# A two-layer decoder trunk on one core: values products set three score blocks back, the norm factors' read-back queued behind transposes, a second raw weight buffer, and the value bounds summed in two slices

## The chip, the core and the metric

The kernel runs on one core of a Trainium2 chip. TensorE (PE) does the matrix products, VectorE (DVE), ScalarE (ACT) and GpSimd (POOL) the elementwise work, and SyncE (SP) issues every DMA of this kernel from one queue. Each engine takes its instructions strictly in the order in which they stand, so an instruction that waits holds up all that is behind it, and that goes for SP's queue of DMAs too. The metric is the device time of the whole program in microseconds, median of three runs, lower is better.

## The reference, cut to what matters

```python
def short_conv_mixer(h, w_in, w_out, conv_w):          # layer 0
    b_gate, c_gate, u, z = jnp.split(h @ w_in, 4, axis=-1)
    conv = causal_conv3(c_gate * u, conv_w)
    return (b_gate * conv * jax.nn.silu(z)) @ w_out

def diff_attn_mixer(h, w_in, w_out, ...):              # layer 1: 8 heads, each of two maps
    q, k, v, z = jnp.split(h @ w_in, 4, axis=-1)
    ...
        logits = jnp.einsum('bqhd,bkhd->bhqk', q_blk, k) * scale
        logits = jnp.where(dist >= 0, logits + bias, -jnp.inf)
        p = jax.nn.softmax(logits, axis=-1)            # 16 maps
        a = p[:, :, 0] - lam * p[:, :, 1]
        o = jnp.einsum('bhqk,bkhe->bqhe', a, v)
        return rmsnorm(o, subln_g) * (1.0 - lambda_init)
    ...
    return (o * jax.nn.silu(z)) @ w_out

for i in range(2):                                     # then a final rmsnorm
    x = x + (short_conv_mixer, diff_attn_mixer)[i](rmsnorm(x, norm_g[i]), ...)
```

The sequence has 1024 tokens, the model 1024 features, all in float32.

## The kernel before, in words

Activations lie with features on partitions, as eight chunks of 128 features by 1024 tokens. A float32 product is taken as three products of high and low parts (`mm3`, line 125: `wh*xh`, `wh*xl`, `wl*xh`). A weight unit of 128 x 1024 is loaded as `wr` (SP), rounded to `wh` by ACT (line 118), and `wl = wr - wh` is left to POOL (line 119); there is one `wr` buffer, and two each of `wh` and `wl`.

Layer 0 (lines 207 to 376) is one long run of products. Layer 1 works head by head. For a head h and a query block b of 128 queries, called block (h,b) below, `scores` (line 489) does this: PE takes the scores of both maps against the keys 0 to (b+1)*128 (line 511); DVE adds the bias (514) and takes the row maximum (516); ACT takes the exponentials into `p1` and `p2` (518); DVE joins the two maps (525); ACT rounds the result to a float16 high part (530, 531 or 534), and POOL (532, for b of 5 and more) or DVE (535) leaves the low part; SP issues one transposing DMA of both (537), out of `p2`'s memory into `p1`'s. `p1` comes from a ring of five slots, `p2` from a ring of three. The score banks in PSUM are two.

`values` (540) takes a group of two blocks: PE multiplies the transposes with the values' high and low parts into the one bank `av` (551), and DVE moves it to `o` (556). After two groups, `head_norm` (558) computes the norm factors of 512 tokens: ACT squares `o` (562), POOL splits the squares (146, 147), PE sums them over the partitions (`cps`, 156), DVE and POOL make the factor `rr` (567, 568), and it goes through memory: SP writes 512 single elements to `rrd` (571) and reads them back to every partition as `rb` (573); POOL multiplies `o` by `rb` (575), two blocks of scores later in the program.

Beside the attention of head h, the projections of the next head fill PE: k and q (`proj_qk`), the gate z of the last head (`proj_z`, whose store of `o` to `yd` at line 406 frees `o`'s slot; there are two), and the values of the next pair of heads (`proj_v`, whose first part bounds each value feature by a sum of squares in `aux`, lines 446 to 463). The instructions are put in order when the program is built, by a list scheduler with priorities (attention stands 4000 ahead of the projections) that simulates the engines' times. So the order on each engine is fixed, and a projection's products (a filler, below) stand where the scheduler expected PE to wait. At the end come the output projection, the residual and the final norm.

Of the kernel before, what the change touches and what calls it, by code (L numbers as in the profile page):

```python
# [15 lines left out]
I32 = mybir.dt.int32  # L16
# [20 lines left out]
class Ring:  # L37
    """Slots of one pool, taken in turn."""
# [4 lines left out]
    def tile(self, shape, dtype, name):  # L43
        tag = self.tags[self.n % len(self.tags)]
        self.n += 1
        return self.pool.tile(shape, dtype, tag=tag, name=name)
# [3 lines left out]
def trunk(ctx: ExitStack, tc: tile.TileContext, a: dict, out: bass.AP):  # L50
# [10 lines left out]
    sl = ctx.enter_context(tc.tile_pool(name="sl", bufs=1))      # slots of 4 KB a partition  # L61
# [12 lines left out]
    r_p1, r_p2, r_w = ring("pa", 5), ring("pb", 3), ring("w", 1)  # L74
    y_tags = r_k.tags + r_q.tags + r_v.tags + r_p2.tags
    free = r_z.tags + r_p1.tags + r_w.tags
# [27 lines left out]
    # the tensor engine's clock is up before the first operands are there  # L104
# [6 lines left out]
    def unit(src, dst=None, raw=None, gain=None):  # L111
        """A weight unit [p, k * 128 + f], times a gain by p, as its high and low parts."""
        wr = wp.tile([P, D], F32, tag="wr", bufs=1, name="wr") if raw is None else raw
# [11 lines left out]
    def mm3(ps, wh, wl, rh, rl, ranges, ks=range(KC)):  # L125
        """ps[:, o] (+)= sum_k w[k].T @ r[k][:, t] for the (o, t, size) given."""
# [15 lines left out]
    def bf16_parts(sq, r1, r2, engs):  # L142
        """sq as the exact sum of three bfloat16 parts; the upper half of a float32 is its first 8 bits."""
# [6 lines left out]
    def col_sums(parts, n):  # L150
        """[p, b] = the sum of the parts' column of token b * 128 + p."""
# [8 lines left out]
    def norm_cols(sqs, n, rdst, tmp=None):  # L160
        """rdst[p, b] = rsqrt(mean_d x^2 + eps) of token b * 128 + p, from column sums of sqs."""
# [9 lines left out]
    def spread(r, tiles, eng):  # L171
        """Diagonal blocks of r's high and low parts."""
# [9 lines left out]
    def rows(tiles, n, at=None):  # L182
        """Every partition: the diagonals, one behind the other."""
# [6 lines left out]
    def norm_rows(rsrc, dst, n, tags):  # L190
        """dst[:, t] = r of token t on every partition, n blocks of 128 tokens at most 4 a step."""
# [19 lines left out]
    # the first three units (c, u, z) go k by k as x and they arrive  # L211
# [58 lines left out]
    # units come as (c, u, z, b) of each chunk of 128 features  # L270
# [48 lines left out]
    # relative bias less its far value, by distance + 127; masked past the diagonal  # L319
# [12 lines left out]
    # lambda, and the scale C that keeps the attention differences in float16's range  # L332
# [23 lines left out]
    # output projection, residual, and the split of the next layer's input  # L356
# [223 lines left out]
    def attention(h):  # L580
# [3 lines left out]
        for i, g in enumerate(order(h)):  # L584
# [3 lines left out]
            if i % 2 == 0 and norms:  # L588
                next(norms.pop())
# [165 lines left out]
```

## Time and profile before

| | us |
|---|---|
| device time, median of 3 runs | 1201.77 |
| lowest and highest | 1200.87, 1205.01 |
| span of the profiled execution | 1207.0 |
| layer 0 and its output projection | 0 to 458 |
| norm and first projections of layer 1 | 458 to 494 |
| attention, from the first scores to the last | 494 to 1073 |
| last values, output projection and final norm | 1073 to 1207 |

The profile is of one execution. No time beside its span is given for it, so the span is its own time here; it is 5.2 us (0.4%) above the median of the three runs. A granted clock of 1.0 is 2.4 GHz for TensorE, 0.5 is 1.2 GHz. Waits are read thus: the engine and line that waited, the engine and line that released it, the total, the times, the longest. In the timeline a number in square brackets is the idle time of that engine ahead of the row, with its releaser. SPq is SP's queue.

### The profile page before, as it was taken

Reading aid. Unit: us, or ns where it says so; the run is one execution under the profiler, and the core shown is the slowest. Engines: PE = TensorE matmul, PEld = TensorE weight load, DVE = VectorE, ACT = ScalarE, POOL = GpSimd, SP = SyncE. Lnnn points to the kernel's source line nnn. Section 1 sums busy time; section 2 is a strip of 40 time slices with the busy share of each in tenths; the row PEclk is TensorE's granted clock in tenths of the full one; section 3 lists DMA queues with packets and bytes.
Section 4 is the critical chain, followed back from the end, with each engine's and each line's share of the span. In section 5 each row is a group of like instructions: output and inputs, shape, how many; then the busy total and the mean of one; then the engine's idle time right before and its main releaser. Section 6 shows DMA issues by size and latency. Waiting matters only on the chain.

```text
span 1207.0 us, 15391 instructions
## 1 busy us (share of the span) xinstructions
PE 1072.0 (89%) x5960; PEld 899.9 (75%) x5960; DVE 590.7 (49%) x945; ACT 421.9 (35%) x705; POOL 563.5 (47%) x355
## 2 busy tenths in 40 slices
PE   8899999999999998996789867998879777888987
PEld 6778888888888886886678656886677666666786
DVE  6563222322323224873587636766385652785123
ACT  3211111101112232463464534545345343355232
POOL 7553424424423552464464545546436554443253
PEclk9899999999999998998989989998889888987989
DMA  5211111111113440356263443534545446457222
GB/s 178 85 53 53 53 53 38 50 53 53 48 40 110 157 140 35 95 81 131 60 150 76 101 105 86 128 89 103 120 95 88 97 112 127 101 119 208 53 105 97
DMA packets 124825, 112.41 MB, mean 93 GB/s; under 512 B 89248, under 2 KB 97104, under 8 KB 124752
## 3 DMA queue, kind: packets, MB, share of 16 engines
q1 hardware_dynamic: 124752, 111.42, 36.3%
q8 instruction: 47, 0.77, 0.3%
q14 instruction: 26, 0.21, 0.1%
HBM read 67.82 MB, written 12.12 MB: 66 GB/s over the span
## 4 chain that ended last, share of the span: by engine, by line
PE 56%; DMA 16%; POOL 9%; issue 8%; DVE 7%; ACT 3%; SPq 0%; POOLq 0%; DVEq 0%; ACTq 0%
PE big L131 34%; PE mm L131 14%; DMA rrd<-rr 7%; DMA p<-p 3%; DMA rb<-rrd 3%; PE sc L511 3%; PE av L551 2%; POOL wl L119 1%; POOL p L532 1%; POOL o L575 1%; DVE nm L516 1%; DVE aux L452 1%; POOL acc L660 1%; DMA yr<-yd 1%; DVE p L525 1%
## 5 line engine op out<-in xcount | busy, mean ns | idle before, releaser
L119 POOL TENSOR_TENSOR wl<-wr,wh 128x1024 fp32r<-128x1024 f32 x75 | 184.1, 2454 | 275.6 <-ACT wh L118 270.4
L118 ACT ACTIVATE wh<-wr 128x1024 fp32r<-128x1024 f32 x75 | 79.3, 1058 | 370.5 <-PE big L131 307.6
L131 PE MATMUL mm<-xh,wh 128*128 128x512 f32 (+1 forms) x432 | 172.0, 398 | 13.3 <-ACT xh L627 6.1
L131 PE MATMUL mm<-xl,wh 128*128 128x512 f32 (+1 forms) x432 | 171.6, 397 | 2.2 <-POOL xl L628 2.2
L131 PE MATMUL mm<-xh,wl 128*128 128x512 f32 (+1 forms) x432 | 170.4, 396 | 0.0
L131 PE MATMUL big<-xh,wh 128*128 128x512 f32 x464 | 143.8, 391 | 2.2 <-DVE cr L288 2.2
L131 PE MATMUL big<-xh,wl 128*128 128x512 f32 x464 | 143.7, 390 | 0.0
L131 PE MATMUL big<-xl,wh 128*128 128x512 f32 x464 | 143.5, 391 | 0.0
L551 PE MATMUL av<-p,vt 128*128 128x128 f16 x864 | 72.4, 249 | 69.2 <-DMA p<-p 52.4
L518 ACT ACTIVATE p<-sc,nm 128x256 f32<-128x256 f32 (+7 forms) x128 | 93.8, 736 | 95.9 <-DVE nm L516 80.0
L551 PEld LDWEIGHTS <-vt 128*128 128x128 f16 x864 | 61.9, 113 | 81.0 <-issue 56.1
L131 PEld LDWEIGHTS mm<-xh,wh 128*128 128x128 f32 x432 | 84.7, 196 | 29.3 <-ACT xh L627 6.5
L131 PEld LDWEIGHTS big<-xh,wh 128*128 128x128 f32 x464 | 87.3, 188 | 20.6 <-issue 2.6
L511 PE MATMUL sc<-kt,qt 128*128 128x512 f32 (+2 forms) x384 | 94.0, 368 | 9.6 <-DMA qt<-qt 5.5
L131 PEld LDWEIGHTS big<-xh,wl 128*128 128x128 f32 x464 | 87.6, 189 | 18.2
L131 PEld LDWEIGHTS big<-xl,wh 128*128 128x128 f32 x464 | 87.4, 188 | 18.2
L131 PEld LDWEIGHTS mm<-xl,wh 128*128 128x128 f32 x432 | 84.9, 196 | 18.2 <-POOL xl L628 3.1
L131 PEld LDWEIGHTS mm<-xh,wl 128*128 128x128 f32 x432 | 84.6, 196 | 15.1
L575 POOL TENSOR_TENSOR o<-o,rb 128x512 f32<-128x512 f32 x16 | 20.7, 1294 | 158.0 <-DMA rb<-rrd 145.6
L516 DVE TENSOR_REDUCE nm<-sc 128x2 f32<-128x256 f32 (+5 forms) x96 | 90.7, 950 | 1.1
L511 PEld LDWEIGHTS sc<-kt,qt 128*128 128x128 f32 x384 | 68.9, 201 | 19.9 <-ACT p L518 5.7
L478 PE MATMUL mm<-wl,xh 128*128 128x256 f32 x256 | 73.1, 287 | 1.8 <-POOL wl L119 1.8
(174 smaller groups left out, 1997.7 us busy)
## 6 DMA issues: line engine op xcount, KB each, us to landing
wr<-in_w_in SPq DMA_DIRECT2D x53, 512.0 KB, 3.5
wr<-in_w_out SPq DMA_DIRECT2D x16, 512.0 KB, 4.4
qt<-qt SPq DMA_DIRECT2D x32, 256.0 KB, 3.7
xr<-in_xT SPq DMA_DIRECT2D x15, 512.0 KB, 4.5
wr<-in_w_v SPq DMA_DIRECT2D x14, 512.0 KB, 4.0
x2d<-x SPq DMA_DIRECT2D x8, 512.0 KB, 2.8
kt<-lo SPq DMA_DIRECT2D x32, 128.0 KB, 3.0
rb<-rrd SPq DMA_DIRECT2D x16, 256.0 KB, 5.7
```

The source lines that it names most:

```text
L118: A.activation(out=wh, in_=wr, func=AF.Copy)
L119: G.tensor_tensor(out=wl, in0=wr, in1=f(wh), op=ALU.subtract)
L131: T.matmul(ps[:, o:o + n], lhsT=w[:, s], rhs=r[k][:, t:t + n], start=(k == 0 and r is rh and w is wh), stop=(k == KC - 1 and w is wl))
L452: V.tensor_tensor(out=sq if k == KC - 1 else aux[:, k % 4, :], in0=aux[:, (k - 1) % 4, :], in1=aux[:, k % 4, :], op=ALU.add)
L478: T.matmul(pt[:, i, :], lhsT=xh[k][:, ts], rhs=wl[:, kk], start=False, stop=False)
L511: T.matmul(sc[:, i, c0:c1_], lhsT=qt[:, var, ts], rhs=kt[:, c0:c1_], start=(var == 0), stop=(var == 1))
L516: V.tensor_reduce(out=nm[:, ms], in_=sc[:, :, :L], axis=AX, op=ALU.max, negate=True)
L518: A.activation(out=(p1_, p2_)[m][:, :L], in_=sc[:, i, :L], func=AF.Exp, bias=nm[:, m:m + 1], accum_out=st[:, m:m + 1])
L525: V.scalar_tensor_tensor(out=p1_[:, :L], in0=p2_[:, :L], scalar=cs[:, 1:2], in1=p1_[:, :L], op0=ALU.mult, op1=ALU.add)
L532: G.tensor_tensor(out=al, in0=p1_[:, :L], in1=ah, op=ALU.subtract)
L551: T.matmul(av[:, qi * P:(qi + 1) * P], lhsT=v[:, kb, es], rhs=at[:, r, :], start=(kb == 0 and r == 0 and v is vh), stop=(kb == qb and v is ...
L575: G.tensor_tensor(out=o, in0=o, in1=rb, op=ALU.mult)
```

## The change

Four things are changed, all in layer 1; comments and docstrings are also gone, so line numbers move by one to some twenty.

- `values` and what hangs on it (the norm steps) become `attend`, which is called when the first block of the second group after is scored, and its products are tied on PE behind the last score product of that block (`issue_after` adds an order on the same engine, no wait on another). So three blocks of scores stand between a group's last block and its values. The last two groups are attended after the last head's scores, with the same priority.
- The read-back of `rb` is issued at the second norm step, behind the last transposing DMA that the program has issued by then, in place of directly behind the write of `rrd`.
- `wr` has a second buffer from the start of layer 1 to the output projection, in the 4 KB that `aux` had.
- `aux` is two slices, not four: the running sum stays in slice 0, each new square goes to slice 1. It shares the slot `dgl` with a norm tile, and its result `srow` has a slot of its own.

```diff
@@ Ring.tile
-        return self.pool.tile(shape, dtype, tag=tag, name=name)
+        pool, tag = tag if isinstance(tag, tuple) else (self.pool, tag)
+        return pool.tile(shape, dtype, tag=tag, name=name)
...
-    r_p1, r_p2, r_w = ring("pa", 5), ring("pb", 3), ring("w", 1)
+    r_p1, r_p2, r_wr = ring("pa", 5), ring("pb", 3), Ring(wp, ["wr0"])
     y_tags = r_k.tags + r_q.tags + r_v.tags + r_p2.tags
-    free = r_z.tags + r_p1.tags + r_w.tags
+    free = r_z.tags + r_p1.tags + [(wp, "wr1")]
...
@@ unit
-        wr = wp.tile([P, D], F32, tag="wr", bufs=1, name="wr") if raw is None else raw
+        wr = r_wr.tile([P, D], F32, name="wr") if raw is None else raw
...
@@ ahead of layer 1
+    r_wr.tags.append("wr1")
     heads = [dict() for _ in range(NH)]
...
@@ proj_v
-            aux = r_w.tile([P, 4, 256], F32, name="aux")
+            aux = sm.tile([P, 2, 256], F32, tag="dgl", name="aux")
             sq = sm.tile([P, 256], F32R, tag="sqw", name="sq")
             for k in range(KC):
-                A.activation(out=aux[:, k % 4, :], in_=f(ws[k // 4][0])[:, (k % 4) * 256:(k % 4 + 1) * 256],
+                A.activation(out=aux[:, min(k, 1), :], in_=f(ws[k // 4][0])[:, (k % 4) * 256:(k % 4 + 1) * 256],
                              func=AF.Square, scale=g_sb[:, 1, k:k + 1])
                 if k:
-                    V.tensor_tensor(out=sq if k == KC - 1 else aux[:, k % 4, :], in0=aux[:, (k - 1) % 4, :],
-                                    in1=aux[:, k % 4, :], op=ALU.add)
+                    V.tensor_tensor(out=sq if k == KC - 1 else aux[:, 0, :], in0=aux[:, 0, :], in1=aux[:, 1, :], op=ALU.add)
...
-            srow = aux[:, 0, :]
-            half = aux[:, 1, :].bitcast(I32)            # half of n's biased exponent
+            srow = sm.tile([P, 256], F32, tag="srow", name="srow")
+            half = aux[:, 1, :].bitcast(I32)
...
-            sd = aux[:, 2, :].rearrange("p (a b) -> p a b", b=P)
+            sd = aux[:, 0, :].rearrange("p (a b) -> p a b", b=P)
...
+    turned = []
@@ scores
-                        T.matmul(sc[:, i, c0:c1_], lhsT=qt[:, var, ts], rhs=kt[:, c0:c1_],
-                                 start=(var == 0), stop=(var == 1))
+                        hd["last", qb] = T.matmul(sc[:, i, c0:c1_], lhsT=qt[:, var, ts], rhs=kt[:, c0:c1_],
+                                                  start=(var == 0), stop=(var == 1))
...
-        dma(out=at[:, :2 * qb + 2, :], in_=p16[:, :2 * L], transpose=True)
+        turned.append(dma(out=at[:, :2 * qb + 2, :], in_=p16[:, :2 * L], transpose=True))
...
@@ head_norm
             dma(out=rrd[h, half].rearrange("(b p) -> p b", p=P), in_=rr)
+        yield
+
         rb = sm.tile([P, 512], F32, tag="dgh", name="rb")
-        dma(out=rb, in_=rrd[h, half].unsqueeze(0).partition_broadcast(P))
-        yield
+        with tc.issue_after(turned[-1].ins):
+            dma(out=rb, in_=rrd[h, half].unsqueeze(0).partition_broadcast(P))
         G.tensor_tensor(out=o, in0=o, in1=rb, op=ALU.mult)
         yield
 
-    norms = []
+    norms, behind = [], []
+
+    def attend(h, i, g):
+
+        values(h, g)
+        if i % 2 == 0 and norms:
+            next(norms.pop())
+        if i % 2:
+            norms.append(head_norm(h, g // 2))
+            next(norms[-1])
...
@@ attention
                 scores(h, g, qi)
-            values(h, g)
-            if i % 2 == 0 and norms:
-                next(norms.pop())
-            if i % 2:
-                norms.append(head_norm(h, g // 2))
-                next(norms[-1])
+
+                if qi == 0 and len(behind) == 2:
+                    with tc.issue_after(heads[h]["last", 2 * g].ins):
+                        attend(*behind.pop(0))
+            behind.append((h, i, g))
...
@@ behind the last head
+    with tc.high_priority(offset=AHEAD):
+        while behind:
+            attend(*behind.pop(0))
     next(norms.pop())
...
+    r_wr.tags.pop()
-    wtags = [None] * 4 + r_v.tags[:2] + q7 + r_k.tags[2:] + r_w.tags + r_p2.tags
+    wtags = [None] * 4 + r_v.tags[:2] + q7 + r_k.tags[2:] + [(wp, "wr1")] + r_p2.tags
...
```

What the scheduler makes of it is seen in the order of the built programs. POOL around the low part of block (2,7), the last of head 2 (`p_4978` before, `p_4942` now; `rr` and `o<-o,rb` are the norm of its first half); before:

```order
L532 TENSOR_TENSOR p_4948<-p_4947,p_4948 128x896
L568 TENSOR_TENSOR rr<-rr,neghalf 128x4
L119 TENSOR_TENSOR wl<-wr,wh 128x1024
L430 TENSOR_TENSOR lo<-tq,kt 64x512
L575 TENSOR_TENSOR o<-o,rb 128x512
L532 TENSOR_TENSOR p_4978<-p_4977,p_4978 128x1024
L437 TENSOR_TENSOR qt<-tq,qt 64x512 x2
```

and now:

```order
L535 TENSOR_TENSOR p_4866<-p_4865,p_4866 128x896
L571 TENSOR_TENSOR rr<-rr,neghalf 128x4
L439 TENSOR_TENSOR qt<-tq,qt 64x512 x2
L535 TENSOR_TENSOR p_4942<-p_4941,p_4942 128x1024
L120 TENSOR_TENSOR wl<-wr,wh 128x1024
L439 TENSOR_TENSOR qt<-tq,qt 64x512 x2
L407 TENSOR_TENSOR o<-o,th 128x512
L120 TENSOR_TENSOR wl<-wr,wh 128x1024
L535 TENSOR_TENSOR p_5345<-p_5344,p_5345 128x896
L407 TENSOR_TENSOR o<-o,th 128x512
L580 TENSOR_TENSOR o<-o,rb 128x512
```

The multiplication by `rb` stood ahead of the block's low part; it now stands behind it, with six further rows between.

SP at the same place, where `p_4977` (before) and `p_4941` (now) are the transposes of block (2,7); before:

```order
L537 DMA_TRANSPOSE p_4947<-p_4948 128x14x128
L571 DMA rrd<-rr 128x4x1
L573 DMA rb<-rrd 128x512
L114 DMA wr<-in_w_v 128x1024
L431 DMA kt<-lo 64x512 x2
L537 DMA_TRANSPOSE p_4977<-p_4978 128x16x128
L438 DMA qt<-qt 64x2x512 x2
```

and now:

```order
L540 DMA_TRANSPOSE p_4865<-p_4866 128x14x128
L574 DMA rrd<-rr 128x4x1
L440 DMA qt<-qt 64x2x512 x2
L540 DMA_TRANSPOSE p_4941<-p_4942 128x16x128
L115 DMA wr<-in_w_in 128x1024
L440 DMA qt<-qt 64x2x512 x2
```

The read-back `rb` stood directly behind the write `rrd`, ahead of a weight load, two moves of `kt` and the transposes. Now the transposes follow the write, and this factor's read-back is the eighth row behind it, behind the transposes of block (3,6).

PE ahead of the values of these blocks, `mm` being a filler; before, block (2,7):

```order
L131 MATMUL mm<-xh_2322,wh 128x512
L131 MATMUL mm<-xl_2330,wh 128x512
L131 MATMUL mm<-xh_2322,wl 128x512
L131 MATMUL mm<-xh_2323,wh 128x512
L551 LDWEIGHTS vt
L551 MATMUL av<-p_4977,vt 128x128
```

and now, where the group's first block (2,6) is `p_4865`:

```order
L132 MATMUL mm<-xh_2326,wh 128x512
L132 MATMUL mm<-xl_2334,wh 128x512
L132 MATMUL mm<-xh_2326,wl 128x512
L514 MATMUL sc<-kt,qt 128x384 x2
L514 MATMUL sc<-kt,qt 128x256 x2
L554 LDWEIGHTS vt
L554 MATMUL av<-p_4865,vt 128x128
```

Before, the values stood behind fillers with no later scores between; now they stand right behind a score product of block (3,4), and blocks (3,6) and (3,7) are scored in between.

## Rows read from the trace of the kernel before

**Rows 1.** The page: busy time of each engine, span, instructions.

```profile
PE 1072.0 (89%) x5960; PEld 899.9 (75%) x5960; DVE 590.7 (49%) x945; ACT 421.9 (35%) x705; POOL 563.5 (47%) x355
```

**Rows 2.** Stretches: us, busy of five engines, clock, DMA share, GB/s.

```profile
73.00:370.00 297.00, 296.07 (x1299) 244.41 (x1299) 91.72 (x96) 44.48 (x48) 115.81 (x66) 0.99 0.15 48
480.00:1140.00 660.00, 555.06 (x3503) 470.32 (x3502) 399.35 (x718) 302.09 (x550) 328.15 (x215) 0.92 0.47 105
```

**Rows 3.** Waits of PE, whole span: us, times, longest.

```profile
PE av L551 <- DMA p<-p: 52.4, 10, 11.2
PE av L551 <- DVE o L556: 16.6, 3, 6.5
```

**Rows 4.** Waits of SP's queue, 480 to 1140.

```profile
SPq L573 <- DMA rrd<-rr: 127.9, 16, 9.6
SPq L114 <- POOL wl L119: 64.4, 21, 5.8
```

**Rows 5.** Waits of POOL, 480 to 1140.

```profile
POOL o L575 <- DMA rb<-rrd: 145.6, 15, 14.8
```

**Rows 6.** Timeline 682 to 714, block (2,7): start, us, engine, operation [idle before].

```profile
682.55 1.16 PE L511 MATMUL sc<-kt,qt 128*128 128x512 f32 x4
...
689.95 0.57 SPq L571 DMA_DIRECT2D rrd<-rr  x1
...
693.24 1.06 ACT L531 ACTIVATE p<-p 128x1024 f16<-128x1024 f32 x1
...
699.51 0.33 SPq L573 DMA_DIRECT2D rb<-rrd  x1
...
705.28 1.26 POOL L575 TENSOR_TENSOR o<-o,rb 128x512 f32<-128x512 f32 x1 [12.10 <-DMA rb<-rrd]
706.50 2.12 POOL L532 TENSOR_TENSOR p<-p,p 128x1024 f16<-128x1024 f32 x1
...
708.65 1.95 SPq L537 DMA_TRANSPOSE p<-p  x1
...
713.05 1.25 PE L551 MATMUL av<-p,vt 128*128 128x128 f16 x10 [11.16 <-DMA p<-p]
```

**Rows 7.** DMA issues: out<-in, count, KB, median us to landing.

```profile
rb<-rrd SPq DMA_DIRECT2D x16, 256.0 KB, 5.7
...
p<-p SPq DMA_TRANSPOSE x64, 3.8
...
rrd<-rr SPq DMA_DIRECT2D x16, 2.0 KB, 8.8
```

**Rows 8.** Timeline of PE: two products of 256 columns; a block's values.

```profile
805.09 0.28 PE L478 MATMUL mm<-wl,xh 128*128 128x256 f32 x1
805.21 0.28 PE L479 MATMUL mm<-wh,xl 128*128 128x256 f32 x1
...
694.77 1.35 PE L551 MATMUL av<-p,vt 128*128 128x128 f16 x21
```

**Rows 9.** Timeline, blocks (1,5) and (7,7): last scores, and their transposes.

```profile
590.54 0.85 PE L511 MATMUL sc<-kt,qt 128*128 128x512 f32 x4
...
614.05 3.12 SPq L537 DMA_TRANSPOSE p<-p  x2
...
1071.95 1.07 PE L511 MATMUL sc<-kt,qt 128*128 128x512 f32 x4
...
1098.81 1.71 SPq L537 DMA_TRANSPOSE p<-p  x1
```

**Rows 10.** Timeline of SP and PE: a weight load behind a read-back.

```profile
738.98 0.32 SPq L573 DMA_DIRECT2D rb<-rrd  x1
739.40 0.37 SPq L114 DMA_DIRECT2D wr<-in_w_in  x1
...
747.10 0.80 PE L131 MATMUL mm<-xh,wh 128*128 128x512 f32 x1 [3.94 <-ACT wh L118]
```

**Rows 11.** Tile aux, its sums: line, count, ns min/median/max.

```profile
L452 DVE TENSOR_TENSOR aux<-aux x24: 410/502/2102, 482.1 to 888.8; 128x256 f32<-128x256 f32 x24
```

More of the change, by code (lines that the diff above doesn't have):

```diff
@@ L688, in out_unit @@
         if d == len(wo):
-            dst = None if d < 2 else [sl.tile([P, D], F32R, tag=t, name="wo") for t in wtags[2 * d:2 * d + 2]]
+            dst = None if d < 2 else [Ring(sl, [t]).tile([P, D], F32R, name="wo") for t in wtags[2 * d:2 * d + 2]]
             raw = r_yr.tile([P, D], F32, name="wr") if d % 2 else None
```

## The prediction

> **What bounds the kernel now.** The page first: PE is busy for 89% of the span, DVE, POOL and ACT for half or less [rows 1], so PE sets the time and the question is when it is idle or slow. The stretches place that. In layer 0 PE is never idle and the clock is full: 1299 products in 297.0 us, 0.229 us each. From 480 to 1140 it is busy 555.1 of 660.0 us, and the granted clock is 0.92 [rows 2]. So 104.9 us are idle, and 0.08 x 660 = 52.8 us of clock are withheld in the same stretch. PE's waits name two thirds of the idle time: 52.4 us in ten waits of `values` for transposes, 16.6 us in three that the profile puts down to DVE's `o` [rows 3]; together 69.0 us in 13 stalls, 36 us are other waits.
>
> Why the transposes are late is seen in the timeline of block (2,7). Its last scores leave PE at 683.7, ACT has its high part at 694.3, and POOL could take the low part then. But POOL stands at `o<-o,rb` for 12.1 us; `rb` could not land sooner, because SP stood from the write of `rrd` at 689.95 until 699.5 before it issued the read-back. So the low part starts at 706.5, the transposes at 708.65, and PE stands for 11.2 us [rows 6]. Over the attention SP waits 127.9 us in 16 such places, 8.0 us each, with transposes and weight loads queued behind [rows 4], and POOL 145.6 us in 15 [rows 5]. A write of 2 KB takes 8.8 us to land, a read-back 5.7, transposes 3.8 [rows 7]. Block (2,7) is then 29.4 us from its last score to its values, and a stall is what the fillers between don't cover.
>
> **The held values.** No product is added or removed; the values move. I count from the order what PE has to do between a block's last score and its values. A filler of 512 columns costs 0.23 us [rows 2], one of 256 columns 0.12, a value product 1.35 / 21 = 0.06 [rows 8], four score products of 512 columns at most 1.2 [rows 6], in the mean of all widths some 0.85. Before, block (2,7) has 66 fillers and 54 value products behind it: 15.1 + 3.2 = 18.3 us against 29.4. Now it has 110 long fillers, 96 short ones, 54 value products and six maps of scores: 25.2 + 11.5 + 3.2 + 5 = 45 us. That stall goes. Counted the same way, of the 13 stalls those of blocks (0,6), (1,6), (2,7), (3,7), (4,6), (6,2), (6,6) and (7,2) find more work between than they took; (1,7) lacks 1 us.
>
> The hold is not long everywhere, for the scheduler moves fillers to where it expects PE to be idle. Block (1,5) now has 19 us behind it, and took 614.05 - 591.4 = 22.7 us to its transposes [rows 9] and 3.8 more to land [rows 7]: 7.4 short. By the same count (3,5) lacks 7.9, (4,3) 4, (5,5) 3.6, (5,7) 4.8, (6,7) 5.8, (7,5) 2.8, (7,6) 5.4. Block (7,7), the last, has 15.4 us, and took 1098.8 - 1073.0 = 25.8 to its transposes [rows 9]; with 3.8 to land that is 14 short, 9 beyond (7,6). With (1,7) this is 52 us: were every block as slow as now, 69 us of stalls would become 52, a gain of 17. If each lost the 8.0 us that one blocked read-back costs [rows 4], only some 6 at the last block would stay, a gain of 63. I take 18 left, so **51 us** (17 to 63), near the upper end because of the next part.
>
> **The read-back.** The same 16 writes and 16 read-backs are issued. In the order now at least one transposing DMA stands between each write and its read-back except the last pair; in five places the write has also many rows ahead of the read-back, as at block (2,7). So SP stands no longer in front of transposes for 8.0 us: I expect its 127.9 us to fall below 40. What it costs: `rb` lands later, and POOL, which waits for it in order, has after most writes only one to four instructions (1 to 7 us) ahead of the multiplication. POOL's 145.6 us [rows 5] will stay near 130; only the low parts that matter, as that of (2,7), now stand ahead of it. Behind it stand `wl` and norm steps, which fillers need later.
>
> The Trainium skill's page "DMA: Bandwidth & Descriptors", section "Latency and other measured facts", gives about 2 us as the fixed cost of a DMA. By that SP would stand some 32 us in all, and moving the read-back would return a quarter as much; the trace has 8.8 us for this write, and decides.
>
> **The second buffer.** SP also waits 64.4 us in 21 places for POOL's `wl`, before it may load the one `wr` again [rows 4]; with two it waits for the unit before. These waits lie in front of transposes too, and are part of the 51. One stall is of its own: a load stood behind a read-back until 739.4 and PE stood 3.94 us at 747.1 [rows 10]. That gives **4 us** (0 to 4).
>
> **The bounds in place.** Four times eight squares and seven sums; each square now waits for the sum before it. A sum takes 0.50 us [rows 11], so 28 of them add up to 14 us in which ACT may stand, beside a PE that has fillers. Cost **1 us** (0 to 5), and 5 if the first value products of a pair wait for it.
>
> **The clock.** Idle time brings the low clock. In proportion, 52.8 us x 55 / 104.9 = 28 us of withheld clock go with 55 us of idle time, but part of what is withheld lies over the idle time itself. I take **15 us** (0 to 28).
>
> **New waits.** When PE no longer stands, the other engines have the same work in less time: POOL has 328 us of work and some 130 of waits in what would be 600, not 660. The nearest row is the 36 us of other waits of PE that are there now; they may vanish in part or double. I take **12 us** more (0 to 36).
>
> **Sum.** 51 + 4 + 15 - 1 - 12 = 57 us. The profiled execution would have 1207.0 - 57 = 1150 us of span; against the median of 1201.8 that is 1145 us. The forecast's own range is 1110 to 1175: at its slow end the held values give 30 and the clock 6 (30 + 4 + 6 - 1 - 12 = 27), at its fast end 63 and 28 with 2 of new waits (92).
>
> **Rivals.** (a) *The latencies stay.* If blocks take as long as now, since POOL still stands 145 us, the stalls move to the ten blocks with the short hold: 17 + 4 + 5 of clock - 1 - 12 = 13 us, so 1189. For it: the shorter counts; against it: the low part of every block of 7 now stands ahead of `rb` on POOL.
>
> (b) *POOL becomes the bound, and the kernel is slower.* The read-back stands behind a transposing DMA, and that may itself wait for its block. POOL's stage is 328 us of work and 15 waits [rows 2, 5]; it fills 660 us when a wait reaches 22 us, against 9.7 now, and the least it can be with nothing between is 8.8 + 5.7 = 14.5 [rows 7]. At 25 us each it is 703, 43 more than now: 1245. Against it: where the read-back stands far behind the write, POOL's own row does so too.
>
> (c) *The slots bind, and nothing is gained.* A `p1` slot is now held from the exponential until values that stand three blocks on, and there are five as before; `p2` has three. From the first scores at 494 to the last ones' end at 1073 a block takes 579 / 64 = 9.0 us. A loop over five slots is as slow as that when a slot is held 45 us; (2,7) holds it about 32 (29.4 and its own value products). So the hold must grow by 13 us beyond what the slowest blocks take now, for a time of 1200.
>
> The page "Perfetto Trace Analysis", section "Optimization Strategy", of the Trainium skill says that the same bubble repeated on the saturated engine can mean too few buffers; by that rule holding slots longer without a sixth would move the bubble to the exponentials, which is (c). No long wait of ACT for a slot is in the trace.
>
> (d) *All goes.* 63 + 4 + 28 and no new wait: 95 us, 1107.
>
> **How the numbers follow.** The forecast has 0.60, (a) 0.19, (b) 0.10, (c) 0.06, (d) 0.05. That the change does not do what it says has no share of its own: the order shows the values and the read-backs moved. For 8 in 10, the range leaves out (b) and half of (d), and takes in (a): 1107 to 1196. A measurement of this kernel tells about 0.3%, 3.6 us, from no change: faster by more than that are the forecast, (d), nearly all of (a) and a little of (c), 0.85; within it 0.06; slower (b) in the main, 0.09.
>
> **What would show it.** PE's waits of `values` for transposes should be 10 to 25 us in total, SP's for `rrd` below 40, the clock from 480 on 0.94 or more, POOL's for `rb` near 130. Stalls, if any, should be at (7,6) and (7,7) and at blocks 5 of odd heads. The last scores should end near 1016 us, and the stretch from there to the end should stay within 10 us of the 134 it takes now. I am wrong if POOL's waits grow past 220 us, if ACT's exponentials wait for slots, or if fillers wait for `wl` in place of the values.

## The result, and the profile after

The changed kernel takes 1167.2 us (median of 4 runs, 1163.8 to 1168.5) against 1202.9 on the same chip for the kernel before (4 runs): a ratio of 0.971, interval 0.9685 to 0.9738. The gain is 36 us; 57 were forecast. The profiled execution is 40.3 us shorter in its span, 1166.7 against 1207.0.

From the page of the kernel after (busy time, share of the span, instructions of each engine), which answers to [rows 1]:

```profile
span 1166.7 us, 15388 instructions
PE 1060.6 (91%) x5960; PEld 893.4 (77%) x5960; DVE 605.6 (52%) x945; ACT 425.4 (36%) x705; POOL 573.3 (49%) x355
```

TensorE has the same 5960 products. It is 11.4 us less busy, since the same products ran at a higher clock, and idle for 1166.7 - 1060.6 = 106.1 us instead of 135.0. These 28.9 and 11.4 us are the whole difference. By stretches (us, busy time of five engines, clock, DMA share, GB/s), against [rows 2]:

```profile
73.00:370.00 297.00, 296.27 (x1299) 244.69 (x1300) 91.71 (x95) 44.66 (x48) 115.64 (x66) 0.99 0.16 48
480.00:1140.00 660.00, 581.08 (x3791) 499.90 (x3791) 427.45 (x743) 326.86 (x587) 362.09 (x232) 0.94 0.52 111
```

Nothing moved in layer 0; from 480 to 1140 the clock is 0.94 instead of 0.92. TensorE's waits over the whole span (total, times, longest), against [rows 3]; the last two rows are of the kernel before:

```profile
PE av L554 <- DMA p<-p: 24.3, 4, 11.1
PE sc L514 <- DMA qt<-qt: 21.5, 6, 6.6
PE cps L157 <- ACT sqo L565: 15.4, 4, 6.0
PE sc L511 <- DMA qt<-qt: 5.5, 3, 2.3
PE cps L156 <- ACT sqo L562: 6.0, 2, 4.5
```

The 69.0 us of waits of the values are 24.5 now (0.2 of them for DVE's `o`). Two others have come in: scores that wait for the exchange of `q`, 21.5 us against 5.5 before, and column sums that wait for ScalarE's squares, 15.4 against 6.0. So 44.5 us went, 16.0 and 9.4 came, and the rest of the idle time fell by 9.8.

The sync queue and GpSimd, 480 to 1140, against [rows 4, 5]:

```profile
SPq L115 <- POOL wl L120: 75.2, 23, 7.9
SPq L579 <- DMA rrd<-rr: 41.8, 11, 9.1
POOL o L580 <- DMA rb<-rrd: 114.9, 14, 13.6
```

The queue's waits for `rrd` fell from 127.9 to 41.8 us. Those for `wl` did not fall, although there are two buffers now. GpSimd still stands 114.9 of its 145.6 us. And the block that [rows 6] followed, (2,7), in the timeline after:

```profile
683.38 1.74 SPq L574 DMA_DIRECT2D rrd<-rr  x1
686.52 2.15 POOL L535 TENSOR_TENSOR p<-p,p 128x1024 f16<-128x1024 f32 x1
688.70 5.90 SPq L540 DMA_TRANSPOSE p<-p  x1
712.60 1.08 SPq L579 DMA_DIRECT2D rb<-rrd  x1
717.38 1.42 POOL L580 TENSOR_TENSOR o<-o,rb 128x512 f32<-128x512 f32 x1 [4.64 <-DMA rb<-rrd]
```

The read-back stands 29 us behind its write, so `rrd` has long landed (this is a good case: in five of the 16 places the read-back stands 18 to 32 us behind its write, in the other eleven 8 to 11); the low part follows its high part at once; the transposes are issued 14 us behind the block's last score (674.6) where it took 25 before. The values start at 728.4 and wait for nothing.

### The profile page after: what moved, and what is told of

Its sections match the earlier page's. It is cut to its first block, busy times and chain, and to the rows that moved or that the text cites. A ratio compares the mean times of both kernels' runs of the same rounds, so it can differ in the third digit from the quotient of the medians.

```text
span 1166.7 us, 15388 instructions
## 1 busy us (share of the span) xinstructions
PE 1060.6 (91%) x5960; PEld 893.4 (77%) x5960; DVE 605.6 (52%) x945; ACT 425.4 (36%) x705; POOL 573.3 (49%) x355
## 4 chain that ended last, share of the span: by engine, by line
PE 60%; DMA 12%; POOL 10%; issue 8%; DVE 5%; ACT 3%; SPq 1%; POOLq 0%; DVEq 0%; ACTq 0%
PE big L132 35%; PE mm L132 14%; PE sc L514 4%; DMA qt<-qt 3%; DMA rrd<-rr 3%; POOL wl L120 3%; PE av L554 2%; PE mm L479 2%; DMA wr<-in_w_out 2%; PE mm L480 2%; PE mm L478 2%; POOL qt L439 1%; DMA rb<-rrd 1%; DMA p<-p 1%; POOL p L535 1%
## 5 line engine op out<-in xcount | busy, mean ns | idle before, releaser
L514 PE MATMUL sc<-kt,qt 128*128 128x512 f32 (+2 forms) x384 | 93.1, 366 | 23.3 <-DMA qt<-qt 21.5
L554 PE MATMUL av<-p,vt 128*128 128x128 f16 x864 | 59.2, 229 | 24.8 <-DMA p<-p 24.3
L580 POOL TENSOR_TENSOR o<-o,rb 128x512 f32<-128x512 f32 x16 | 20.6, 1286 | 123.5 <-DMA rb<-rrd 114.9
L554 PEld LDWEIGHTS <-vt 128*128 128x128 f16 x864 | 53.0, 103 | 30.5 <-issue 18.2
```

The lines of the kernel that those rows point to most:

```text
L514: hd["last", qb] = T.matmul(sc[:, i, c0:c1_], lhsT=qt[:, var, ts], rhs=kt[:, c0:c1_], start=(var == 0), stop=(var == 1))
L554: T.matmul(av[:, qi * P:(qi + 1) * P], lhsT=v[:, kb, es], rhs=at[:, r, :], start=(kb == 0 and r == 0 and v is vh), stop=(kb == qb and v is ...
L580: G.tensor_tensor(out=o, in0=o, in1=rb, op=ALU.mult)
```

## The experiments

All ratios are to the kernel before, timed beside each kernel on the same chip (its medians there were 1208.8, 1210.3, 1202.0 and 1208.3 us). One thing holds for all of them: a scheduler orders the instructions, so an edit also shifts where fillers and transfers far from it are issued, and a difference between two kernels holds both.

### Which part carries it

My theory was that of the forecast: the hold takes the stalls away, the read-back adds to that by taking the standing out of the sync queue, and each would give a good part of the gain alone. The rival: the one is worth nothing without the other.

**Without the hold** (`values` again behind the scores of its own group):

```diff
-                if qi == 0 and len(behind) == 2:
-                    with tc.issue_after(heads[h]["last", 2 * g].ins):
-                        attend(*behind.pop(0))
-            behind.append((h, i, g))
+            attend(h, i, g)
```

> The changed kernel without the hold: a group's values follow its own two blocks of scores again; read-back behind transposes, two wr and the bounds in place stay. My theory (the hold covers a block's way, the read-back shortens it, both are needed): the stalls of values for transposes come back in part, 40 to 55 us where the changed kernel has 24 and the kernel before 69, SP's waits for rrd stay below 60 us, and the time is 1180 to 1195 us. Rival, the read-back does it alone: 1172 or less with stalls below 30. Rival, the hold does it alone: 1200 or more with stalls near 69.

Measured: 1214.7 us, ratio 1.003 (1.0009 to 1.0055), slower than I expected.

```profile
PE av L554 <- DMA p<-p: 54.8, 9, 11.0
SPq L579 <- DMA rrd<-rr: 100.8, 13, 9.2
```

The values wait for transposes as before. But the read-back is hardly held here: in 11 of the 16 places no transposing DMA is issued between the write and its read-back (in the changed kernel, in one), and most of the queue's standing is left. So the edit of the read-back gives nothing without the hold; what a queue without the standing would give without the hold, this run does not show.

**The read-back at once**, behind its write:

```diff
+        rb = sm.tile([P, 512], F32, tag="dgh", name="rb")
+        dma(out=rb, in_=rrd[h, half].unsqueeze(0).partition_broadcast(P))
         yield
-
-        rb = sm.tile([P, 512], F32, tag="dgh", name="rb")
-        with tc.issue_after(turned[-1].ins):
-            dma(out=rb, in_=rrd[h, half].unsqueeze(0).partition_broadcast(P))
```

> The changed kernel with the read-back issued directly behind its write, as before; hold, two wr and bounds in place stay. My theory: SP's waits for rrd are near 128 us again (41.8 in the changed kernel), blocks take as long as before, the stalls of values move to the blocks with a short hold, 40 to 55 us in all, and the time is 1180 to 1195 us. Rival, the hold does it alone: stalls near 24 and 1163 to 1172. Rival, the read-back does it alone: 1200 or more.

Measured: 1227.5 us, ratio 1.014 (1.0106 to 1.0175): slower than before. I had expected 40 to 55 us of stalls of the values; they wait 26.5 us for transposes, and the scores wait for `q`:

```profile
PE sc L514 <- DMA qt<-qt: 44.8, 6, 13.7
```

**The hold alone**, put into the kernel before (`attend` does what stood in the place of the first line, a few lines further up):

```diff
-            values(h, g)
...
+                if qi == 0 and len(behind) == 2:
+                    with tc.issue_after(heads[h]["last", 2 * g].ins):
+                        attend(*behind.pop(0))
+            behind.append((h, i, g))
```

> The kernel before with the hold alone: read-back at once, one wr, bounds in four slices. My theory: as the prediction's case in which the latencies stay, stalls of values 40 to 55 us and 1183 to 1195 us. Rival, the hold carries all: 1163 to 1172. Rival, holding slots without shortening anything gains nothing: 1198 to 1206, with waits of ACT's exponentials for transposes over 20 us.

Measured: 1232.3 us, ratio 1.017 (1.0142 to 1.0203): slower as well. Yet the hold does what it should. TensorE's waits in this kernel:

```profile
PE sc L513 <- DMA qt<-qt: 50.3, 5, 11.8
PE mm L132 <- ACT xh L640: 16.5, 2, 12.5
PE sc L513 <- ACT p L520: 16.3, 3, 7.0
PE av L553 <- DMA p<-p: 16.1, 2, 8.1
PE mm L478 <- POOL wl L120: 13.4, 2, 8.0
```

Waits of the values for transposes are down to 16.1 us. In their place scores wait for `q`, 50.3 us in five stalls, all at a head's first scores; in four of the five the exchange is issued within 5 us behind a standing of the queue for `rrd`. The other rows are waits that came or grew beside them. One of the five in the timeline (start, us, engine, operation [idle before and what ended it]):

```profile
543.60 0.38 SPq L573 DMA_DIRECT2D rrd<-rr  x1
554.36 0.33 SPq L575 DMA_DIRECT2D rb<-rrd  x1
554.79 1.54 SPq L539 DMA_TRANSPOSE p<-p  x1
556.42 1.90 SPq L439 DMA_DIRECT2D qt<-qt  x2
545.46 3.58 POOL L438 TENSOR_TENSOR qt<-tq,qt 64x512 fp32r<-64x512 f32 x2
557.73 1.26 POOL L577 TENSOR_TENSOR o<-o,rb 128x512 f32<-128x512 f32 x1 [8.69 <-DMA rb<-rrd]
561.13 1.83 PE L513 MATMUL sc<-kt,qt 128*128 128x512 f32 x4 [11.75 <-DMA qt<-qt]
```

GpSimd has the low parts of `q` ready at 549.0. Their exchange is issued at 556.4, since the queue stood from 544.0 to 554.4 for `rrd`. TensorE stands 11.75 us. The hold has taken the values off the list of what is late, and the same standing strikes the next transfer in the queue that TensorE needs, for which there is nothing to hold it back.

**Hold and read-back**, without the other two edits (one raw-weight buffer, the four slices of the bounds); to the kernel with the hold alone this adds

```diff
-        rb = sm.tile([P, 512], F32, tag="dgh", name="rb")
-        dma(out=rb, in_=rrd[h, half].unsqueeze(0).partition_broadcast(P))
         yield
+
+        rb = sm.tile([P, 512], F32, tag="dgh", name="rb")
+        with tc.issue_after(turned[-1].ins):
+            dma(out=rb, in_=rrd[h, half].unsqueeze(0).partition_broadcast(P))
```

> The two instruction-moving edits together, with before's single buffer of raw weights and before's four-slice bounds of V. If the gain of the whole change comes from these two edits acting together, the ratio to the kernel before is 0.965 to 0.978 (about 1165 to 1180 us), the waits of TensorE for transposes stay near 20 to 30 us against 69 before and the sync queue's waits for rrd under 50 us. If the in-place bounds or their memory carry a part of it, the ratio is above 0.985.

Measured: 1193.5 us, ratio 0.985 (0.979 to 0.991). Together the two gain, but only half of what the whole change does.

**One raw-weight buffer**, all else as changed:

```diff
-    r_wr.tags.append("wr1")
...
-    r_wr.tags.pop()
```

> The changed kernel with one wr in layer 1, as before; hold, read-back and bounds in place stay. My theory: the second buffer is worth little, since SP's waits for wl were 64.4 us before and are 75.2 in the changed kernel: 1165 to 1175 us. Rival, the second buffer carries the gain by freeing SP: SP's waits for wl over 100 us and 1185 or more.

Measured: 1175.5 us, ratio 0.971 (0.9679 to 0.9749), the ratio of the whole change. The second buffer is worth nothing that can be measured (the queue's waits for `wl` are 84.2 us with one, 75.2 with two).

**The bounds in place alone**, in the kernel before (the lines cut are those of the change):

```diff
-            aux = r_w.tile([P, 4, 256], F32, name="aux")
+            aux = sm.tile([P, 2, 256], F32, tag="dgl", name="aux")
...
-            srow = aux[:, 0, :]
+            srow = sm.tile([P, 256], F32, tag="srow", name="srow")
```

> The kernel before with the bounds of V summed in place and nothing else. The prediction took 1 us for them. With hold and read-back together, the in-place bounds took the ratio from 0.985 to 0.971 by way of another order of issue. If they are worth something by themselves, the ratio here is 0.983 to 0.993 too; if what they gave there was the order that the other edits happen to get with them, it is 0.995 to 1.006 here.

Measured: 1207.9 us, ratio 1.004 (1.0021 to 1.0061). By themselves they lose a little. But one buffer with the bounds in place has 0.971, and hold with read-back without them 0.985: there they are worth some 1.4%. The largest stall that only the latter has is one of 13.7 us; its rows:

```profile
756.76 0.58 SPq L573 DMA_DIRECT2D rrd<-rr  x1
757.43 1.23 SPq L539 DMA_TRANSPOSE p<-p  x1
765.73 0.34 SPq L578 DMA_DIRECT2D rb<-rrd  x1
767.10 4.93 SPq L539 DMA_TRANSPOSE p<-p  x2
773.26 0.37 ACT L520 ACTIVATE p<-sc,nm 128x128 f32<-128x128 f32 x1 [12.05 <-DMA p<-p]
```

One transposing DMA stands between write and read-back, which is too little: the queue stands again, two transposes wait behind it, and an exponential waits 12.05 us for the `p` slot that they are to free. In the kernel with the bounds in place two transposes fall between at this place and the queue stands for 4 us. What I can show is that this standing is there in the one and shorter in the other; that the bounds bring this about by anything but the order that comes out, I can't, and it stays open.

### Where the standing happens

My theory: it is the sync queue's standing in front of `q` by which the hold alone loses. The rival: GpSimd's standing at `o<-o,rb`. **The hold alone with write and read-back issued from GpSimd's queue**, so that the sync queue never stands for them and GpSimd stands as long as before:

```diff
-            dma(out=rrd[h, half].rearrange("(b p) -> p b", p=P), in_=rr)
+            G.dma_start(out=rrd[h, half].rearrange("(b p) -> p b", p=P), in_=rr)
...
-        dma(out=rb, in_=rrd[h, half].unsqueeze(0).partition_broadcast(P))
+        G.dma_start(out=rb, in_=rrd[h, half].unsqueeze(0).partition_broadcast(P))
```

> The hold alone (1232 us where it was timed, 1.017 of before, with 141 us of waits for rrd on the sync queue and 50 us of waits for qt on TensorE), with the write of rr and its read-back issued from GpSimd's queue instead of the sync queue; GpSimd still stands until rb is there. Theory that the sync queue's standing in front of q's exchanges is what the hold alone loses by: sync waits for rrd vanish, waits for qt fall to under 20 us, and the ratio falls to 0.965 to 0.985. Rival, that GpSimd's standing at the product o loses it: waits for qt stay above 35 us and the ratio stays above 1.00.

Measured: 1202.8 us, ratio 0.994 (0.9925 to 0.9964). Between both expectations.

```profile
PE sc L513 <- DMA qt<-qt: 26.2, 5, 7.5
POOL rb L575 <- DMA rrd<-rr: 130.0, 15, 12.4
POOL o L577 <- DMA rb<-rrd: 30.0, 11, 5.6
```

The waits for `q` halve, from 50.3 to 26.2 us, and 2.3% come back. GpSimd stands 130.0 + 30.0 = 160 us, as it did with the hold alone (157.4). So issuing the trip from the sync queue cost the hold alone all of its 1.7% and a little more. Why it gains no more than 0.6% when the sync queue no longer stands is not shown here: GpSimd's standing, which still holds low parts, is one candidate, and the landing of the write, told with the last run below, another.

**The whole change from GpSimd's queue** (the same edit):

> The whole change with the write of rr and its read-back issued from GpSimd's queue, the read-back still held behind the transposes. The sync queue loses its 42 us of waits for rrd. Theory that what is left in the changed kernel (21.5 us of waits for qt, 24.3 for transposes) is still the sync queue standing: the ratio to the kernel before falls from 0.971 to 0.955 to 0.967. Rival, that GpSimd now stands instead and holds low parts: its waits for rrd and rb exceed 130 us and the ratio is 0.972 to 0.99.

Measured: 1196.6 us, ratio 0.995 (0.993 to 0.9963). The gain is nearly gone, and GpSimd stands:

```profile
POOL rb L579 <- DMA rrd<-rr: 78.3, 10, 11.2
POOL o L580 <- DMA rb<-rrd: 28.3, 12, 5.0
POOL rb L579 <- PE sc L514: 26.8, 3, 10.1
```

But the edit does more than I meant it to. `issue_after` orders instructions of one engine, the transposes are issued from the sync queue and the read-back now from GpSimd's, so nothing holds the read-back any more: all 16 stand 9 to 12 us behind their write. (The third row's read-backs too stand 9 to 11 us behind their writes, so what ended these waits is probably the landing of the write, not the scores named.) The run is thus the hold alone from GpSimd's queue with the bounds in place and a second buffer, and its ratio is that of the run above (0.994) within a thousandth. What a held read-back would cost on GpSimd it does not show.

**The whole change with layer 1's raw weights loaded from GpSimd's queue**, to take away the 75.2 us that the sync queue stands for `wl`:

```diff
-        dma(out=wr, in_=src)
+        (G.dma_start if layer1 else dma)(out=wr, in_=src)
...
+    layer1 = True
...
+    layer1 = False
```

> The whole change with layer 1's raw weights loaded from GpSimd's queue. Between 480 and 1140 us the sync queue of the changed kernel stands 75.2 us (23 times) before such a load, until GpSimd has read the buffer. Theory that this standing holds transposes and q's exchanges behind it: the waits for transposes and for qt on TensorE fall by 15 us or more together and the ratio to 0.95 to 0.965. Rival, that it stands there when nothing behind it is due: waits as before, GpSimd some 20 us busier with issuing, ratio 0.970 to 0.985.

Measured: 1216.7 us, ratio 1.010 (1.0066 to 1.0136). TensorE waits 40.1 us for `q` and 33.4 for transposes, longer than in the changed kernel, where it is 21.5 and 24.3. The wait itself did not move: from 480 to 1140 GpSimd stands 0.9 us at these loads for its own `wl`. Issuing takes it some 0.6 us for each of 34, some 20 us in all. Whether that is what costs the time no run shows; both expectations missed.

**The low part of map 1's `q` on VectorE:**

```diff
-                        G.tensor_tensor(out=qt[own[m], 1, :], in0=tq[own[m]], in1=f(qt)[own[m], 0, :], op=ALU.subtract)
+                        (G, V)[m].tensor_tensor(out=qt[own[m], 1, :], in0=tq[own[m]], in1=f(qt)[own[m], 0, :], op=ALU.subtract)
```

> The change with the low part of map 1's q on VectorE instead of GpSimd, as the keys have it. Theory that GpSimd's queue holds q back at a head's first scores: TensorE's waits of scores for qt fall from 21.5 us to 5 to 12, and the ratio falls to 0.955 to 0.968. Rival, that the exchange DMA and its place in the sync queue hold q, not GpSimd: waits for qt stay at 15 to 30 us and the ratio at 0.968 to 0.978 (VectorE takes on some 16 subtractions of 64x512).

Measured: 1183.4 us, ratio 0.978 (0.9744 to 0.9814). Waits for `q` are 26.9 us, no shorter. So the work on GpSimd is not what makes `q` late in the changed kernel.

**`rb` in memory of its own**, with one raw-weight buffer:

```diff
-        rb = sm.tile([P, 512], F32, tag="dgh", name="rb")
+        rb = wp.tile([P, 512], F32, tag="wr1", name="rb")
```

> The change with one raw-weight buffer, the read-back tile rb in the memory of the second instead of the slot that it shares with the squares sqo. Theory that the shared slot makes a new limit: ScalarE's waits of sqo for the product o (31 us in the changed kernel) go to nearly nothing, the column sums' waits for sqo on TensorE (15.4 us) fall below 4, and the time falls by 5 to 15 us, to a ratio of 0.960 to 0.967 against 0.971. Rival, that the squares wait beside other work or something else is late next: the ratio stays between 0.968 and 0.975.

Measured: 1178.1 us, ratio 0.974 (0.9702 to 0.9784). ScalarE's squares no longer wait for GpSimd's `o`, and TensorE's sums wait 1.3 us for the squares instead of 6.9 with one buffer and 15.4 in the changed kernel, but no time is gained: TensorE waits 27.4 us for `q` (27.5 with one buffer), and its sums 9.1 us for their second parts (3.5). The shared slot made a wait that something else replaces.

### The trip itself

All edits so far move the wait for the trip through memory. The last one leaves **the trip out**, in the kernel with one raw-weight buffer. `spread` writes a high and a low part of `rr` on the diagonals of 128 x 128 blocks, and `rows` multiplies these by a matrix of ones, which puts every value on all partitions; the kernel has both for the norms of the layers' inputs:

```diff
-        with nc.allow_non_contiguous_dma(reason="512 single elements"):
-            dma(out=rrd[h, half].rearrange("(b p) -> p b", p=P), in_=rr)
+        dgs = wp.tile([P, 2, 4, P], F32R, tag="wr1", name="dgn")
+        dgs = dgs[:, 0], dgs[:, 1]
+        spread(rr, dgs, V)
         yield
-        rb = sm.tile([P, 512], F32, tag="dgh", name="rb")
-        with tc.issue_after(turned[-1].ins):
-            dma(out=rb, in_=rrd[h, half].unsqueeze(0).partition_broadcast(P))
-        G.tensor_tensor(out=o, in0=o, in1=rb, op=ALU.mult)
+        bps = rows(dgs, 4)
+        V.tensor_tensor(out=o, in0=o, in1=bps, op=ALU.mult)
```

> The change with one raw-weight buffer, and the trip of rr through memory left out altogether: rr goes into diagonal blocks on VectorE (in the memory that the second raw-weight buffer had), two matmuls of 512 columns with a matrix of ones bring it to every partition behind the next pair's values, and VectorE multiplies the outputs straight from PSUM. Neither the sync queue nor GpSimd waits for rrd or rb any more (37.5 and 108.2 us with one buffer, 41.8 and 114.9 in the changed kernel). Theory that what is left of the waits for qt and transposes (21.5 and 24.3 us in the changed kernel, 27.5 and 14.7 with one buffer) is this standing: they fall to 20 us or less together and the ratio to the kernel before is 0.945 to 0.963. Rival, that the change has already taken this trip off the path and the waits that are left have other causes: ratio 0.966 to 0.98, with VectorE some 35 us busier. A ratio above 0.985 would say that VectorE is late with scores instead.

Measured: 1117.1 us, ratio 0.924 (0.921 to 0.9269): below the theory's own range, and 0.047 below the change. The page, the added instructions (median of 32 diagonal blocks' halves, of 32 matmuls, of 16 products), and all waits of TensorE above 3.2 us:

```profile
PE 1057.1 (95%) x5992; PEld 891.2 (80%) x5992; DVE 647.3 (58%) x1025; ACT 423.8 (38%) x705; POOL 552.9 (50%) x339
L180 DVE TENSOR_TENSOR dgn<-ident,rh x32: 664/684/2874, 544.7 to 1037.0; 128x512 fp32r<-128x512 f32 x32
L188 PE MATMUL bps<-dgn,ones_r x32: 390/397/795, 571.0 to 1041.1; 128*128 128x512 f32 x32
L578 DVE TENSOR_TENSOR o<-o,bps x16: 666/680/689, 571.9 to 1041.6; 128x512 f32<-128x512 f32 x16
PE sc L513 <- ACT p L520: 11.4, 3, 5.6
PE sc L513 <- DMA qt<-qt: 7.5, 3, 4.4
PE bps L188 <- DVE o L558: 5.5, 1, 5.5
PE big L132 <- DVE xl L236: 3.5, 2, 2.3
```

TensorE's waits for transposes are no longer listed, those for `q` are 7.5 us, and the idle time is 1114.1 - 1057.1 = 57.0 us against 106.1 in the changed kernel. TensorE has 32 more matmuls and is yet 3.5 us less busy, as the clock rose again (0.97 over the span instead of 0.95); VectorE is 41.7 us busier than in the changed kernel, beside TensorE. The last scores end at 999.2 instead of 1033.8, and the stretch behind them takes 114.9 us instead of 132.9. One wait that goes there is ScalarE's, in the changed kernel, where the squares of the output's norm use the slot that the last `rb` still holds:

```profile
ACT sq L674 <- POOL o L580: 21.1, 1, 21.1
```

It was there before too (20.9 us). But it is not what these 18 us were: with `rb` in memory of its own it is gone as well, and the stretch takes 129.2 us there against 126.3 with one buffer. The stall of 11.1 us at block (7,7), the last, lies in this stretch of the changed kernel; it is gone with one buffer already, so 11.4 of the 18 us have no single wait to their name.

**What the trip still costs in the changed kernel** is seen in the times of landing. There 37 transfers are issued while a write of `rr` is on its way, and none of them lands before the write has. The seven exchanges of `q` among them take a median of 8.3 us to land and the 16 transposing DMAs 7.7; the other 25 and 48 take 4.1 and 3.4. It is no different from another queue: in the whole change from GpSimd's queue, 32 are issued from the sync queue during a write, and only two land first, both issued within 0.3 us of it. So the write delays what is issued behind it even where no queue stands. One write and the two exchanges behind it in the changed kernel (count, ns that issuing takes, start; time to landing), and the scores that wait for them:

```profile
L574 SPq DMA_DIRECT2D rrd<-rr x1: 1742/1742/1742, 683.4 to 683.4; - x1
DMA to landing us min/median/max: 10.8/10.8/10.8
L440 SPq DMA_DIRECT2D qt<-qt x2: 610/622/635, 685.2 to 686.5; - x2
DMA to landing us min/median/max: 8.3/8.7/9.1
694.45 1.83 PE L514 MATMUL sc<-kt,qt 128*128 128x512 f32 x4 [6.17 <-DMA qt<-qt]
```

The write lands at 694.1, the first exchange at 694.3. Three of the four longest waits for `q`, 13.7 of the 21.5 us, end so, and all four stalls of the values have such a write ahead of them: the transposes of (1,5) and (3,5) are issued during one and take 8.9 and 8.4 us to land, those of (5,7) stand in the queue behind a read-back that waits for one, and at (7,7) ScalarE stands 7.5 us between its two steps of the block for a weight load that was issued 0.6 us behind one and took 10.9 us:

```profile
1054.95 1.15 ACT L122 ACTIVATE wo<-wr,gsub 128x1024 fp32r<-128x1024 f32 x1 [7.51 <-DMA wr<-in_w_out]
```

No run changes the write alone, so this rests on the times of landing and on what went when the trip was left out.

## Why the prediction was right in sign and 22 us short

**The sum.** In the spans 57 us were forecast and 40.3 came. By terms: held values and second buffer 55, measured 44.5 (waits of the values 69.0 to 24.5); clock 15, measured 11.4 (TensorE's busy time); bounds and new waits 13 against, measured 15.6 against (16.0 + 9.4 - 9.8). The errors are 10.5, 3.6 and 2.6, 16.7 in all. The values' term holds most of it: I took 18 us of stalls left, and 24.5 are; the second buffer's 4 are the rest of the 10.5. The count took 3.8 us for the transposes to land wherever they stand. The 16 that are now issued during a write take 7.7, and the stalls at (1,5) and (3,5), 3.5 and 2.7 us, are shorter than that difference.

**Where the stalls stand.** The count of fillers foretold stalls at (1,5), (3,5), (5,7) and (7,7); those are the four in the trace after, with 3.5, 2.7, 7.1 and 11.1 us. It also foretold short ones at (1,7), (4,3), (5,5), (6,7), (7,5) and (7,6), which did not come; why is not shown block by block. The last scores end at 1033.8 where I had 1016; the stretch behind them takes 132.9, within the 10 us of 134 that I gave.

**The step that failed** is the bookkeeping by parts, and the sum came near for a reason that is not the forecast's. I gave the held values 51 us, the read-back no term of its own, and the second buffer 4. On the chip the hold alone costs 1.7%, the read-back's edit without the hold gains nothing (and hardly moves the read-back), and only both together gain. That the sum of the parts lay near is to that extent luck. I had written that the read-back would let the latencies fall and so protect the hold; I had not asked what the hold does to the queue if the latencies stay. Rival (a) gave 13 us of gain for a hold with the latencies left as they are; the two kernels with the hold and the read-back at once lose 1.4 and 1.7%, 17 and 21 us. My count was of the blocks' values alone. The scores wait for `q`, which goes through the same queue, and I had listed what is queued behind the read-back as "transposes and weight loads".

**The second buffer** was given 4 us and has none that shows (0.971 with one and with two). The queue's waits for `wl` went from 64.4 to 75.2 us, and are 84.2 with one buffer and the rest of the change.

**The bounds** were given 1 us of loss. Alone they lose 0.4% (0.2 to 0.6), 5 us, the end that I had kept for the range; together with the others they go with a gain of 1.4%, which I had no term for and can't explain beyond the order.

**The rivals.** (b) fell: GpSimd stands 114.9 us, not more than before. (c) fell in the changed kernel: exponentials wait 15.7 us for slots in all (4.1 before); but the hold and read-back alone show one such wait of 12.05 us, so the mechanism was there, one transposing DMA away. (d) fell for this change. Its 1107 was the price of all stalls of the values and the clock; the kernel without the trip comes near it, at 1117, but 18 us of that are in the stretch behind the last scores, of which I had counted only the stall at (7,7).

**What I took for harmless.** GpSimd's wait for `rb` was to stay near 130 us, and is 114.9; I gave it no price once the low parts that matter stand ahead of it. When the trip is left out, this wait, the sync queue's 41.8 us and the landings behind a write go, and 49 us of TensorE's idle time with them. Which of the three gives most no run separates.

## What to carry to other kernels

A transfer that waits at the head of a queue which all others share is paid by whatever comes next in it: before holding work back, list every kind of transfer behind the wait, for taking one victim away makes the next one late, and the hold can cost time. In the trace, look at when transfers land and not only at when they are issued: here a small write of single elements delayed what was issued behind it from either queue, and no order of issue tried here took that away. Issuing from the queue of an engine that computes lost time in both tries on the changed kernel, though neither shows by what; leaving the trip out, with some hundred short instructions, most on an engine that has room, gave more than all rearranging. Parts of a change are not terms of a sum when they share a queue: test each alone and both together.

## What the runs showed of the hardware that I had not expected

- The 2 KB write of single elements takes 8.8 us to land from the sync queue before, 9.8 in the changed kernel and 10.6 from GpSimd's queue (the hold alone): a tuned order does not shorten it. The 256 KB read-back takes 3.4 to 5.7.
- While such a write was on its way, other transfers did not land: none of 37 issued during one in the changed kernel, and from the sync queue beside a write from GpSimd's two of 32, both issued within 0.3 us of it. With this the exchange of `q` goes from 3.7 us to land before to 5.1 in the changed kernel, and to 3.6 without the trip.
- Issuing a transposing DMA takes a median of 1.3 us on the sync queue in the changed kernel, but 5.90 us at 688.70 in the rows of block (2,7) above, close behind a write of `rr` and two exchanges of `q`. It ends at 694.6, just behind their landing; no run shows whether it waits for one of them.
